# Four split pieces of projection weights, made at other places and in other scratch tiles

## The chip, the cores and the metric

One core of a Trainium2 chip runs the whole kernel. The metric is device microseconds (us) of one execution, and lower is better. The kernel before takes 2753.55 us, the median of three runs (2752.94 to 2757.86).

## The reference

One layer of a streaming encoder over 2048 tokens of width 1024, all in float32. Cut to what matters here:

```
xn = rms_norm(x, mix_norm_g)
aq|ak|av|mq|mk|mv|mo|i|f|ga|gm = xn @ w_in
A = chunk_band_attention(aq, ak, av, rel_bias)          # own chunk and 8 before, 8 heads of 64
M = sigmoid(mo) * rms_norm(mlstm_chunkwise(silu(conv(mq|mk)), mv, i, f))   # 4 heads of 128
y = sigmoid(ga) * (A @ w_att_proj) + sigmoid(gm) * (M @ w_mlstm_proj)
x = x + y @ w_out
x = x + relu(rms_norm(x) @ w_up)^2 @ w_down
out = rms_norm(x)
```

## The kernel before

**Products.** A float32 product is made of three matmuls on a high and a low part of each operand (high x high, high x low, low x high). So every weight tile is split ahead of its use: ScalarE casts the tile to the high part (L685), VectorE subtracts that from the tile (L687). The result lies in one of three tiles `wsp`. The raw tile comes over the SP queue (L583, L644) into one of four tiles `wraw`. Activations are split likewise (L1654 or L1656 on ScalarE, L1659 or L1661 on VectorE) into tiles `r`.

**Quads.** Most large products are done in groups called quads: seven products instead of eight of a two by two block product, with sums and differences of the weight blocks as operands. One quad is 7 weight tiles of 24 matmuls each (L853). PE adds products into shared banks, so between them the copies L2289 (ScalarE, bank to a `ctx` tile) and the sums L2297 (VectorE) must have read a bank before PE writes it again. The sums of weight blocks are made either on the way (L704) or ahead of time by `sum_w` (L560, its subtraction is L575), which loads four pieces into four `ctx` tiles and stores the sums to the tensor `wsum`.

**Order of the program.** The sequence comes from `dense` (L956). The 2048 tokens are four blocks of 512; the first span holds blocks 0 and 1, the second blocks 2 and 3. With the times of the profiled execution:

- 0 to 489 us: input products of blocks 0 and 1, attention and the recurrence of these blocks between them.
- 489 to 640 us: four quads of gates (`GATES`).
- 640 to 775 us: the projections of block 1 (L768 to L770), whose merge with the gates (L1450 loads a gate over SP, L1458 and L1468 multiply and add on VectorE) feeds the output quads; then two output quads (L2511 adds their banks to x).
- 775 to 1201 us: eleven quads of input products of blocks 2 and 3 (`IN_ORDER`).
- 1201 to 1501 us: eight quads of the up projection of the first span (`after_up`).
- 1501 to about 1976 us: the down projection of the first span (L768 to L770), with attention (L1845, L1876, L1818) and the recurrence of blocks 2 and 3 between its matmuls.
- from 1976 us: `project_quads` (L1225), the projections of blocks 2 and 3, which reads split weights ready made from DRAM (`load_split`, L586); then the output, up and down quads of the second span.

**The four pieces.** `project_quads` needs the seven split operands of two quads. They are made long before by `sum_split` (L594) in four pieces: two quads, each in two halves of the columns. One piece loads four 128x512 blocks into four `ctx` tiles (L602), makes four differences on VectorE (L612), and for each of seven operands runs `split_keep` (L628): it takes two scratch tiles, casts the high part on ScalarE (L634), subtracts the low part on VectorE (L636), and stores both to DRAM (tensors `wsplit`, L2550); a scratch tile is free again when its store has landed. The table `KEPT_SUMS` (L64) says at which quad a piece is begun: -4 to -1 are the four gate quads, 0 to 10 the input quads, 11 to 18 the up quads. The pieces have a low priority, so they run where the engines have room.

**Pools.** `ctx` has 16 tiles and serves almost everything: block sums, loads, bank copies. `sc` has 4 tiles (two scores tiles for each half of an attention head). Attention uses `sc` until about 440 us and again from about 1540 us; between these, `sc` serves `norm_mid` (L555), which squares the residual stream for the second norm (load L2584, square L2586 on ScalarE, sum L2590 on VectorE), 16 tiles in the first span; its result is needed at 1347 us.

**The order on each engine.** A planner (`Flow`) walks through all threads with costs and priorities and hands out the tiles; a second pass (`Order`) lists the recorded instructions anew, each engine by due times, with margins for transfers. Each engine then runs its list in order. So the table and the pool of the scratch tiles reach far beyond their own instructions: whoever takes a tile later waits for whoever had it before.

Of the kernel before, what the change touches and what calls it, by code (L numbers as in the profile page):

```python
# [60 lines left out]
ORDER = (0, 1, 3, 2, 5, 4, 6)  # L61
PLAIN, APART = (0, 1, 2, 3, 4, 5, 6), (0, 2, 3, 1, 5, 4, 6)
CHAIN = (1, 0, 3, 5, 6, 2, 4)
KEPT_SUMS = {-4: (0, 0), -3: (0, 1), 8: (1, 0), 17: (1, 1)}  # L64
N_RING = 8
LAST = (3, 1)

# [149 lines left out]
def act_ns(n, ps=False, ap=0):  # L217
    return (51 if ps else 93) + 0.834 * n + 93 * ap


def dve_ns(n):
    return 70 + 1.042 * n
# [162 lines left out]
class Layer:  # L385
# [242 lines left out]
    def split_keep(self, x, n, h, read):  # L628

        fl = self.fl  # L630
        got = yield "get", self.ctx, 2
        hi, lo = (t[:, :512] for t in got)
        yield "act", act_ns(512)
        self.nc.scalar.copy(hi.bitcast(F32R), x)  # L634
        yield "dve", dve_ns(512)
        self.nc.vector.tensor_sub(lo.bitcast(F32R), x, hi)  # L636
        fl.set(read)
        for y, (t, u) in enumerate(zip(got, (hi, lo))):
            fl.spawn(self.store(self.ws[n].ap().bitcast(F32)[:, y, h * 512:h * 512 + 512], u,
                                self.ws_ev[n][2 * h + y], self.ctx, t), 3)  # L640

    def split_w(self, i, src, raw, sent=None, keep=None):
        yield "sp", 1750, 2000
# [312 lines left out]
    def dense(self):  # L956
# [59 lines left out]
        for i, name in enumerate(GATES):  # L1016
            if i - 4 in KEPT_SUMS:
                q, h = KEPT_SUMS[i - 4]
                fl.spawn(self.sum_split(Q_P + q, h), 3)
# [16 lines left out]
        for i, name in enumerate(IN_ORDER):  # L1036
            if i in KEPT_SUMS:
                q, h = KEPT_SUMS[i]
                fl.spawn(self.sum_split(Q_P + q, h), 3)
# [12 lines left out]
        for s in range(NS):  # L1052
# [7 lines left out]
            for i in range(N_F):  # L1060
                if s == 0 and len(IN_ORDER) + i in EARLY_SUMS:
                    fl.spawn(self.sum_w(EARLY_SUMS[len(IN_ORDER) + i]), 3)
                if s == 0 and len(IN_ORDER) + i in KEPT_SUMS:
                    q, h = KEPT_SUMS[len(IN_ORDER) + i]
                    fl.spawn(self.sum_split(Q_P + q, h), 3)
# [1985 lines left out]
```

## Time and profile before

| | us |
|---|---|
| median of the runs | 2753.55 |
| the profiled execution | 2757.34 |
| its span on the core | 2755.5 |
| PE busy | 2739.9 (99%) |
| VectorE busy | 2069.5 (75%) |
| ScalarE busy | 1509.4 (55%) |
| clock of PE granted over the span | 0.998 |

PE is busy for all but 15.6 us of the span, and some 8 us of these lie outside the stretch from 480 to 2100 us. A busy PE does not mean that PE is at its peak, since matmuls overlap and a matmul at a lower clock is busy for longer. A better measure in the stages that hold nothing but matmuls of 512 columns is their count in a window: a full window of 25 us has 112 of them.

### The profile page before, as it was taken

How to read it: one execution, taken by the hardware profiler on the slowest of the kernel's cores; microseconds unless marked ns; L12 is line 12 of the kernel's file. 1: busy time of each engine (PE TensorE's matmuls, PEld its weight loads, DVE VectorE, ACT ScalarE, POOL GpSimd, SP SyncE). 2: the span in 40 equal slices, each digit the busy share in tenths (PEclk: the TensorE clock that was granted, in tenths of full speed). 3: DMA queues.
4: the chain of work that ended last, by engine and by line, in shares of the span. 5: the costliest groups of instructions: out<-in, count | busy, mean ns of one | idle time of the engine just before them, and what ended most of it. 6: DMA issues, size and time to landing. Idle time of an engine off the chain costs nothing.

```text
span 2755.5 us, 38840 instructions
## 1 busy us (share of the span) xinstructions
PE 2739.9 (99%) x13006; PEld 2280.4 (83%) x13006; DVE 2069.5 (75%) x3873; ACT 1509.4 (55%) x2665; POOL 52.9 (2%) x101
## 2 busy tenths in 40 slices
PE   9999999999999999999999999999999999999999
PEld 7888888888778888887888888888888888888888
DVE  7795798777996767876677788889898656555566
ACT  5664576644454545584556565566435655554444
POOL 0010001000000000000000000000000000000000
PEclk9999999999999999999999999999999999999999
DMA  8977759889756589489889998987967667776564
GB/s 291 290 227 251 234 168 309 282 278 340 243 205 233 172 301 328 142 273 320 285 312 312 313 287 254 269 252 248 329 243 260 210 220 258 237 248 220 194 221 163
DMA packets 339417, 704.09 MB, mean 256 GB/s; under 512 B 37992, under 2 KB 68880, under 8 KB 337424
## 3 DMA queue, kind: packets, MB, share of 16 engines
q1 hardware_dynamic: 339072, 701.60, 77.0%
q8 instruction: 102, 1.67, 0.3%
q14 instruction: 99, 0.81, 0.1%
q10 hardware_dynamic: 144, 0.01, 0.0%
HBM read 483.60 MB, written 217.86 MB: 255 GB/s over the span
## 4 chain that ended last, share of the span: by engine, by line
PE 97%; DMA 1%; DVE 1%; ACT 0%; issue 0%; SPq 0%; POOL 0%; ACTq 0%
PE bank L853 45%; PE bank L768 12%; PE bank L770 12%; PE bank L769 12%; PE bank L884 3%; PE bank L1258 3%; PE bank L1845 2%; PE bank L1818 2%; PE bank L1876 2%; PE bank L2131 0%; PE bank L2132 0%; PE bank L2116 0%; PE bank L2130 0%; DMA r<-mfar 0%; PE bank L935 0%; DMA tmp<-mixa 0%
## 5 line engine op out<-in xcount | busy, mean ns | idle before, releaser
L853 PE MATMUL bank<-r,wsp 128*128 128x512 f32 x5544 | 1268.1, 390 | 6.0 <-ACT ctx L2289 3.5
L853 PEld LDWEIGHTS bank<-r,wsp 128*128 128x128 f32 x5544 | 1040.7, 188 | 225.5 <-ACT ctx L2289 3.9
L687 DVE TENSOR_TENSOR wsp<-wraw,wsp 128x1024 fp32r<-128x1024 f32 x442 | 540.0, 1222 | 353.7 <-ACT wsp L685 337.4
L685 ACT CAST wsp<-wraw 128x1024 fp32r<-128x1024 f32 x442 | 465.5, 1053 | 539.8 <-PE bank L853 226.5
L768 PE MATMUL bank<-r,wsp 128*128 128x512 f32 x1328 | 529.2, 399 | 0.0
L769 PE MATMUL bank<-r,wsp 128*128 128x512 f32 x1328 | 519.1, 391 | 0.0
L770 PE MATMUL bank<-r,wsp 128*128 128x512 f32 x1328 | 518.6, 391 | 0.0
L770 PEld LDWEIGHTS bank<-r,wsp 128*128 128x128 f32 x1328 | 249.3, 188 | 53.1
L768 PEld LDWEIGHTS bank<-r,wsp 128*128 128x128 f32 x1328 | 249.6, 188 | 45.4
L769 PEld LDWEIGHTS bank<-r,wsp 128*128 128x128 f32 x1328 | 249.9, 188 | 44.6
L2297 DVE TENSOR_TENSOR ctx<-bank,ctx 128x512 f32<-128x512 f32 x186 | 126.7, 687 | 104.2 <-PE bank L853 101.2
L1659 DVE TENSOR_TENSOR r<-r 128x512 fp32r<-128x512 f32 x251 | 165.8, 687 | 14.3 <-ACT r L1654 14.0
L1654 ACT CAST r<-r 128x512 fp32r<-128x512 f32 x251 | 149.9, 622 | 28.9 <-DMA r<-u 24.6
L2289 ACT COPY ctx<-bank 128x512 f32<-128x512 f32 x186 | 107.8, 582 | 90.6 <-PE bank L853 73.9
L1860 ACT ACTIVATE sc<-sc,scs 128x640 f32<-128x640 f32 (+4 forms) x128 | 97.4, 762 | 75.4 <-DVE scs L1857 69.5
L1851 DVE CUSTOM_DVE_ANT_0 sc<-bank,bias 128x320 f32<-128x320 f32 (+3 forms) x240 | 103.4, 461 | 11.9 <-PE bank L1845 10.5
L1881 DVE TENSOR_TENSOR r<-bank,r 128x512 fp32r<-128x512 f32 (+1 forms) x168 | 97.0, 595 | 20.0 <-ACT r L1879 18.8
L1879 ACT CAST r<-bank 128x512 fp32r<-128x512 f32 (+1 forms) x168 | 82.3, 517 | 48.6 <-PE bank L1876 46.7
L2628 ACT ACTIVATE ctx<-ctx 128x512 f32<-128x512 f32 x96 | 60.5, 630 | 77.2 <-DVE ctx L2297 77.2
L1818 PE MATMUL bank<-r,r 128*128 128x512 f32 x336 | 94.9, 363 | 0.0
L704 DVE TENSOR_TENSOR wraw<-wraw,wraw 128x1024 f32<-128x1024 f32 x76 | 92.3, 1218 | 0.6
L1845 PE MATMUL bank<-r,r 128*128 128x320 f32 (+3 forms) x480 | 85.5, 305 | 0.0
(295 smaller groups left out, 2975.7 us busy)
## 6 DMA issues: line engine op xcount, KB each, us to landing
wraw<-in_wf SPq DMA_DIRECT2D x178, 512.0 KB, 4.8
wraw<-wsum SPq DMA_DIRECT2D x136, 512.0 KB, 4.0
r<-u SPq DMA_DIRECT2D x224, 256.0 KB, 4.3
wraw<-in_w SPq DMA_DIRECT2D x71, 512.0 KB, 5.2
ctx<-in_wf SPq DMA_DIRECT2D x128, 256.0 KB, 5.1
u<-ctx SPq DMA_DIRECT2D x128, 256.0 KB, 3.1
wsum<-ctx SPq DMA_DIRECT2D x112, 256.0 KB, 4.6
u<-tmp SPq DMA_DIRECT2D x96, 256.0 KB, 4.0
```

The costliest lines, as they stand in the source:

```text
L685: nc.scalar.copy(w[:, 0], raw)
L687: nc.vector.tensor_sub(w[:, 1], raw, w[:, 0].bitcast(F32))
L768: mm(ps, lh, rh, start=first, stop=False)
L769: mm(ps, lh, rl, start=False, stop=False)
L770: mm(ps, ll, rh, start=False, stop=last)
L853: mm(ps, wv[:, x, k, n], a[:, y], start=new and k == 0 and x == y == 0, stop=k == 3 and x == 1, skip_group_check=True)
L1654: self.nc.scalar.copy(dst[:, 0], src)
L1659: self.nc.vector.tensor_sub(dst[:, 1], src, dst[:, 0].bitcast(F32))
L1818: nc.tensor.matmul(acc[:, :, c0:c0 + w], st, sl[:, :, o:o + w], start=n == 0, stop=n == total - 1)
L1845: nc.tensor.matmul(bks[x][:, :w], q[:, y, i * P:(i + 1) * P], kf[:, f * P + x * w:f * P + x * w + w], start=y == 0, stop=y == 1)
L2289: nc.scalar.copy(t[:, o:o + 512], ps)
L2297: nc.vector.tensor_add(t[:, o:o + 512], ps, t[:, o:o + 512])
```

## The change

Two things change. The table begins the four pieces at the third gate quad and at the input quads 3, 6 and 8, instead of at gate quads 0 and 1, input quad 8 and up quad 6. And `split_keep` takes its two scratch tiles from `sc` instead of `ctx` (a tile of that pool is a pair, the 640 wide tile and a small one; the first 512 columns of the wide one are used). The four tiles that hold the loaded blocks stay in `ctx`. No instruction is added or taken away.

```
-KEPT_SUMS = {-4: (0, 0), -3: (0, 1), 8: (1, 0), 17: (1, 1)}
+KEPT_SUMS = {-2: (0, 0), 3: (0, 1), 6: (1, 0), 8: (1, 1)}
...
     def split_keep(self, x, n, h, read):
         fl = self.fl
-        got = yield "get", self.ctx, 2
-        hi, lo = (t[:, :512] for t in got)
+        got = yield "get", self.sc, 2
+        hi, lo = (t[0][:, :512] for t in got)
         yield "act", act_ns(512)
         self.nc.scalar.copy(hi.bitcast(F32R), x)
         yield "dve", dve_ns(512)
         self.nc.vector.tensor_sub(lo.bitcast(F32R), x, hi)
         fl.set(read)
         for y, (t, u) in enumerate(zip(got, (hi, lo))):
             fl.spawn(self.store(self.ws[n].ap().bitcast(F32)[:, y, h * 512:h * 512 + 512], u,
-                                self.ws_ev[n][2 * h + y], self.ctx, t), 3)
+                                self.ws_ev[n][2 * h + y], self.sc, t), 3)
```

**First place: the SP queue at the end of the projections of block 1** (about 686 to 704 us). L1450 loads a gate, L644 a raw weight tile, L2214 a block of the output quads' operand, L2498 a block of x. Before:

```order
L644 DMA wraw_64<-in_wf 128x1024
L2214 DMA ctx_121<-yp 128x512
L644 DMA wraw_65<-wsum 128x1024
L1450 DMA tmp_109<-gate 128x512
L1450 DMA tmp_108<-gate 128x512
L2214 DMA ctx_119<-yp 128x512
L644 DMA wraw_67<-wsum 128x1024
L1450 DMA tmp_106<-gate 128x512
L1450 DMA tmp_108<-gate 128x512
```

With the change:

```order
L644 DMA wraw_67<-wsum 128x1024
L1450 DMA tmp_110<-gate 128x512
L1450 DMA tmp_108<-gate 128x512
L644 DMA wraw_66<-wsum 128x1024
L2214 DMA ctx_124<-yp 128x512
L1450 DMA tmp_111<-gate 128x512
L1450 DMA tmp_109<-gate 128x512
L644 DMA wraw_64<-in_wf 128x1024
L2214 DMA ctx_115<-yp 128x512
L2498 DMA ctx_117<-in_xt 128x512
L644 DMA wraw_65<-wsum 128x1024
L2498 DMA ctx_122<-in_xt 128x512
```

The last two gate loads stood behind the raw tile `wraw_67`; now they stand ahead of `wraw_64`, which is three raw weight tiles earlier in the same sequence of weights.

VectorE at the end of the same stage (about 706 to 714 us): L1458 and L1468 merge the last gates, L2227 makes sums of the output quads' operands, L1661 their low parts, L687 that of a weight tile. Before:

```order
L687 TENSOR_TENSOR wsp_62<-wraw_66,wsp_62 128x1024
L2511 TENSOR_TENSOR ctx_113<-bank_134,ctx_113 128x512
L1661 SCALAR_TENSOR_TENSOR r_70<-ctx_117,r_70 128x512
L687 TENSOR_TENSOR wsp_63<-wraw_64,wsp_63 128x1024
L1458 SCALAR_TENSOR_TENSOR tmp_106<-tmp_106,bank_131 128x512
L1458 SCALAR_TENSOR_TENSOR tmp_108<-tmp_108,bank_130 128x512
L1468 TENSOR_TENSOR ctx_126<-tmp_106,tmp_107 128x512
L1468 TENSOR_TENSOR ctx_114<-tmp_108,tmp_111 128x512
L2227 TENSOR_TENSOR ctx_127<-ctx_120,ctx_126 128x512
L2227 TENSOR_TENSOR ctx_123<-ctx_125,ctx_114 128x512
L2227 TENSOR_TENSOR ctx_120<-ctx_121,ctx_120 128x512
```

With the change:

```order
L687 TENSOR_TENSOR wsp_63<-wraw_64,wsp_63 128x1024
L1661 SCALAR_TENSOR_TENSOR r_80<-ctx_113,r_80 128x512
L1661 SCALAR_TENSOR_TENSOR r_81<-ctx_112,r_81 128x512
L1661 SCALAR_TENSOR_TENSOR r_85<-ctx_125,r_85 128x512
L2251 SCALAR_TENSOR_TENSOR tmp_110<-tmp_110,gcol,bias_97 128x512
L2251 SCALAR_TENSOR_TENSOR tmp_111<-tmp_111,gcol,bias_97 128x512
L1468 TENSOR_TENSOR ctx_126<-tmp_107,tmp_106 128x512
L2266 TENSOR_TENSOR tmp_108<-tmp_110,tmp_111 128x512
L2227 TENSOR_TENSOR ctx_120<-ctx_126,ctx_125 128x512
L2251 SCALAR_TENSOR_TENSOR ctx_119<-ctx_119,gcol,bias_96 128x512
L2227 TENSOR_TENSOR ctx_126<-ctx_124,ctx_126 128x512
L1661 SCALAR_TENSOR_TENSOR r_82<-ctx_120,r_82 128x512
```

All L1458 and the other merges (L1468) now stand ahead of the weight tile `wsp_63`; the last merge, `ctx_126`, still stands behind it, and behind three low parts L1661 and two steps (L2251) that normalize x for the input quads.

**Second place: ScalarE in the second up quad** (about 1253 to 1270 us). Before:

```order
L685 CAST wsp_61<-wraw_67 128x1024
L2289 COPY ctx_115<-bank_131 128x512
L2289 COPY ctx_112<-bank_130 128x512
L685 CAST wsp_63<-wraw_64 128x1024
L2289 COPY ctx_126<-bank_133 128x512
L2628 ACTIVATE ctx_126<-ctx_126 128x512
L2632 ACTIVATE ctx_126<-ctx_126 128x512
L2289 COPY ctx_120<-bank_129 128x512
```

With the change:

```order
L685 CAST wsp_63<-wraw_66 128x1024
L2289 COPY ctx_126<-bank_129 128x512
L2289 COPY ctx_113<-bank_132 128x512
L685 CAST wsp_61<-wraw_67 128x1024
L2289 COPY ctx_122<-bank_130 128x512
L2289 COPY ctx_112<-bank_133 128x512
L685 CAST wsp_62<-wraw_65 128x1024
L2289 COPY ctx_127<-bank_129 128x512
```

The bank copies stand about one weight cast earlier, and they go to other `ctx` tiles.

**Third place: ScalarE where the first piece is split** (before about 501 to 505 us, with the change in the third gate quad, about 560 us). Before:

```order
L634 CAST ctx_113<-ctx_123 128x512
L1578 ACTIVATE tmp_110,r_q<-tmp_110 128x512
L2289 COPY ctx_115<-bank_128 128x512
L634 CAST ctx_125<-ctx_119 128x512
L1578 ACTIVATE tmp_107,r_q<-tmp_107 128x512
L685 CAST wsp_62<-wraw_64 128x1024
```

With the change:

```order
L634 CAST sc_98<-ctx_116 128x512
L685 CAST wsp_63<-wraw_64 128x1024
L2289 COPY ctx_117<-bank_130 128x512
L634 CAST sc_102<-ctx_123 128x512
L2289 COPY ctx_113<-bank_133 128x512
L634 CAST sc_98<-ctx_114 128x512
L685 CAST wsp_61<-wraw_66 128x1024
L2289 COPY ctx_127<-bank_129 128x512
```

The scratch of one operand comes back for the next but one: `sc_98` is written again one weight cast later.

The list of each engine changes well beyond these places. On PE the matmuls keep their order, but for single ones, until the end of the up projection; from there on attention and the down projection are interleaved otherwise.

More of the change, by code (lines that the diff above doesn't have):

```diff
@@ L63 @@
 CHAIN = (1, 0, 3, 5, 6, 2, 4)
-KEPT_SUMS = {-4: (0, 0), -3: (0, 1), 8: (1, 0), 17: (1, 1)}
+KEPT_SUMS = {-2: (0, 0), 3: (0, 1), 6: (1, 0), 8: (1, 1)}
 N_RING = 8
@@ L630, in split_keep @@
         fl = self.fl
-        got = yield "get", self.ctx, 2
-        hi, lo = (t[:, :512] for t in got)
+        got = yield "get", self.sc, 2
+        hi, lo = (t[0][:, :512] for t in got)
         yield "act", act_ns(512)
@@ L639, in split_keep @@
             fl.spawn(self.store(self.ws[n].ap().bitcast(F32)[:, y, h * 512:h * 512 + 512], u,
-                                self.ws_ev[n][2 * h + y], self.ctx, t), 3)
+                                self.ws_ev[n][2 * h + y], self.sc, t), 3)
     def split_w(self, i, src, raw, sent=None, keep=None):
```

## The prediction

> **What bounds the kernel now.** I read the busy times first, then PE's waits from 480 to 2100 us (the first piece begins at 473 us, the change's last effect is on the quads after 1976 us), then windows of 25 us.
>
> ```profile
> span 2755.5 us, 38840 instructions
> PE 2739.9 (99%) x13006; PEld 2280.4 (83%) x13006; DVE 2069.5 (75%) x3873; ACT 1509.4 (55%) x2665; POOL 52.9 (2%) x101
> ...
> PE bank L853 <- ACT ctx L2289: 3.5, 1, 3.5
> PE bank L853 <- ACT r L1656: 1.3, 1, 1.3
> PE bank L1553 <- POOL r_far L1585: 0.7, 1, 0.7
> PE bank L1258 <- ACT sc L1296: 0.7, 1, 0.7
> PE bank L853 <- DVE r L1659: 0.5, 1, 0.5
> PE bank L853 <- DVE r L1661: 0.4, 1, 0.4
> PE bank L853 <- DVE tmp L1458: 0.3, 1, 0.3
> ```
>
> PE sets the time. The change takes no matmul away, so it can only win back what PE loses now: seven waits of 7.4 us in all (columns: us in total, times, longest). A wait costs more than its idle time if the clock falls behind it, so I count matmuls in windows (length; then busy us and count of PE, weight loads, VectorE, ScalarE, POOL; granted clock; DMA share; GB/s).
>
> ```profile
> 675.00:700.00 25.00, 25.00 (x112) 20.68 (x111) 20.84 (x33) 11.18 (x16) 0.00 (x0) 1.00 0.68 225
> 700.00:725.00 25.00, 22.98 (x92) 17.86 (x91) 25.00 (x40) 10.85 (x15) 0.00 (x0) 0.93 0.86 299
> 1200.00:1225.00 25.00, 24.53 (x107) 19.75 (x107) 20.79 (x31) 22.14 (x36) 0.00 (x0) 1.00 0.83 278
> 1250.00:1275.00 25.00, 21.54 (x89) 17.37 (x88) 11.48 (x16) 10.79 (x16) 0.00 (x0) 0.93 0.79 268
> 1975.00:2000.00 25.00, 24.91 (x109) 20.00 (x108) 19.77 (x34) 12.24 (x22) 0.00 (x0) 1.00 1.04 410
> 2000.00:2025.00 25.00, 24.31 (x108) 19.81 (x107) 22.32 (x37) 6.37 (x11) 0.00 (x0) 1.00 0.67 240
> ```
>
> A full window has 112 matmuls, so one is worth 25/112 = 0.2232 us. Short of that: 20 matmuls = 4.46 us at 700 us (place C), 5 = 1.12 us at 1200 us (D), 23 = 5.13 us at 1250 us (E), 3 + 4 = 1.56 us at 1975 to 2025 us (F): 12.3 us. The 0.7 us of L1553 (place B, 493 us) come on top. That is the whole prize.
>
> **The change part by part.** The same 28 casts, 28 differences of low parts, 16 differences of blocks, 56 stores (and the loads of the blocks) run in both kernels, so nothing is added or removed:
>
> ```profile
> L634 ACT CAST ctx<-ctx x28: 601/621/663, 501.0 to 1597.0; 128x512 fp32r<-128x512 f32 x28
> L636 DVE TENSOR_TENSOR ctx<-ctx,ctx x28: 671/684/694, 503.9 to 1607.8; 128x512 fp32r<-128x512 f32 x28
> L612 DVE TENSOR_TENSOR ctx<-ctx,ctx x16: 669/686/694, 518.6 to 1580.0; 128x512 f32<-128x512 f32 x16
> L2550 SPq DMA_DIRECT2D wsplit<-ctx x56: 319/405/1052, 501.9 to 1610.5; - x56
> DMA to landing us min/median/max: 2.6/5.2/10.1
> ```
>
> Per piece that is 7 x 0.62 = 4.3 us of ScalarE, 7 x 0.68 + 4 x 0.69 = 7.5 us of VectorE, and 14 x 0.41 = 5.7 us of SP's issue for the stores. Lying beside full PE windows (VectorE 20.84 of 25 us at 675) it costs PE nothing. Without that cover, up to its 7.5 us of VectorE would show. What the change moves is who waits for which tile, so I go by places.
>
> *E, taken as gone: 5.1 us.* The chain of waits there:
>
> ```profile
> 1254.88 0.69 DVE ctx L575
> 1255.59 5.43 DMA wsum<-ctx
> 1261.11 0.59 ACT ctx L2289
> ```
>
> The bank copy L2289 had its bank long before. It waited for its `ctx` tile, which `sum_w` held until a store of 5.43 us had landed; PE stood 3.46 us, and the slower clock behind it makes up the rest of 5.13. In the change two scratch tiles per operand come from `sc` and not from `ctx`, the copies at this place stand one weight cast earlier and go to other tiles, whose former use is, in my reading of the lists, over 4 us done. So I take all 5.1; if another copy meets a tile still being stored, all of it remains (0).
>
> *C, half gone: 2.2 us.*
>
> ```profile
> 703.01 0.32 SPq L1450
> 703.39 3.68 DMA tmp<-gate
> 709.46 1.20 DVE tmp L1458 x2
> 710.65 1.20 DVE ctx L1468 x2
> 712.39 1.28 DVE ctx L2227 x2
> 713.67 0.61 DVE r L1661
> ```
>
> The last gate came at 703.39 + 3.68 = 707.07 us; VectorE then had to merge (two L1458, two L1468) and to form sums and low parts before PE could go on. The load now stands three raw weight tiles earlier. A weight tile feeds 24 matmuls, 24 x 0.2232 = 5.36 us, so it lands some 16 us earlier, and the merges but one stand ahead of the last weight tile's L687. But VectorE is full in this window (25.00 of 25 us), its sum of work is the same, and the last merge stands behind three L1661 and two L2251, some 5 x 0.65 = 3.3 us more. Before, two L1458 and one more L1468 stood there (1.20 + 0.60 = 1.8 us). So the load is no longer last, but VectorE's queue is. Bounds 0 and 4.46; I take half.
>
> The clock at C is a matter of its own:
>
> ```profile
> 712.00:714.00 2.00, 0.73 (x2) 0.30 (x2) 2.00 (x4) 2.00 (x4) 0.00 (x0) 1.00 1.03 401
> 714.00:716.00 2.00, 1.68 (x6) 1.41 (x7) 2.00 (x5) 0.82 (x2) 0.00 (x0) 0.85 1.05 383
> 716.00:718.00 2.00, 2.00 (x6) 1.52 (x6) 2.00 (x5) 1.61 (x4) 0.00 (x0) 0.50 1.04 396
> ```
>
> Waits of 0.3, 1.3 and 0.4 us brought the clock to 0.85 and then 0.50, so 2.0 us of idle time cost 4.46. [...]
>
> *D, half gone: 0.6 us.* PE waited 0.47 us for an operand's low part (L1659), one of many splits that run until 1222 us. In the change all those of the first operands stand ahead of the weight cast at 1214 us. Against it: `norm_mid` needs `sc` as well, and with the pieces there it comes later. Before:
>
> ```profile
> L2586 ACT ACTIVATE sc<-sc x14: 614/628/639, 722.7 to 839.9; 128x512 f32<-128x512 f32 x14
> L2590 DVE TENSOR_TENSOR bias<-bias,sc x14: 681/686/694, 811.3 to 840.6; 128x512 f32<-128x512 f32 x14
> 1175.00:1200.00 25.00, 25.00 (x112) 20.71 (x111) 20.91 (x31) 22.45 (x37) 0.00 (x0) 1.00 0.82 259
> ```
>
> By the lists these 16 squares move from 722 to 840 us to some 1105 to 1224 us: 10.0 us of ScalarE and 11 us of VectorE next to D, where ScalarE has 22.45 of 25 us, while the third piece (4.3 and 7.5 us) leaves it. Bounds 0 and 1.12, half taken. At 800 us the squares leave a full VectorE; no PE wait stands there, so nothing is won.
>
> *B and F: 0.* L1553 comes 20 matmuls earlier at B, as do the steps that feed it; +-0.7. F waits for a copy of `project_quads` itself (L1296), which the change leaves; at best 1.56 are won.
>
> *From 1501 to 1937 us: 0.*
>
> ```profile
> 1501.00:1937.00 436.00, 436.00 (x2362) 373.71 (x2361) 366.13 (x974) 270.30 (x601) 13.76 (x36) 1.00 0.88 271
> 1955.74 0.37 ACT L1825 COPY tmp<-bank 128x256 f32<-128x256 f32 x1 [3.73 <-DVE ctx L2665]
> 1976.03 26.51 PE L1258 MATMUL bank<-r,wsp 128*128 128x512 f32 x114
> ```
>
> The fourth piece leaves this stretch, which is full already and gains nothing. Attention starts later there, and the last L1818 stands 36 matmuls (8.0 us) nearer to the first L1258. Its copy L1825 waited 14 us for its tile before, so that move has cover. Without it, about 4 us would show: 8.0 less the some 4 us that I count between the last operand and its use.
>
> *New waits: 1.7 us of loss.* The lists change everywhere from 490 us on, and each of about a hundred PE windows can meet what happened at E. From none (0) to one more stall of E's size (5.1); I take a third.
>
> **Sum:** 5.1 + 2.2 + 0.6 - 1.7 = 6.2 us. The profiled execution took 2757.34 us (span 2755.5, 1.8 around it) and would come to 2751.1. It stands 3.8 us above the median of the three runs, 2753.55, which gives **2747.3 us**.
>
> **The rivals.**
>
> *Larger gain.* If C to F all go and nothing new comes: 2753.55 - 12.3 = 2741.3, with a small rest 2742.5. For it: PE has no idle time in the full windows at 675 and 1175 us, so stalls are single accidents. Against: VectorE is full at C.
>
> *No change.* `ctx` is used 16 deep and `sum_w` still stores from it; the stall of E comes back at another quad (-7.9 + 5.1) or C remains whole and a late attention tail costs its 4 us (-5.7 + 4): about 2752. For it: what is moved earlier, loads of the pieces included, holds `ctx` tiles at other quads.
>
> *Slower.* Only two pairs of scratch fit into the four `sc` tiles. A pair is held for the cast, the difference and the store, 0.62 + 0.68 + 5.2 = 6.5 us at the median and 11.4 us at the longest landing of 10.1; it is wanted again after one or two weight tiles, 5.4 to 10.7 us. ScalarE runs its list in order, so a cast L634 that waits holds up the bank copies and weight casts queued behind it. PE's cover is one weight tile less a copy and a sum, 5.36 - 1.3 = 4 us. From a landing of about 9 us on, PE waits. If three of four pieces meet one such landing, at E's price: 3 x 5.13 = 15.4 - 7.9 = +7.5, so 2761.0. Waits for stores now (idle before L634, then before L636; us, times):
>
> ```profile
>   DMA gate<-ctx: 3.7, 2
> ...
>   DMA wsplit<-ctx: 1.9, 1
> ```
>
> For it: both wait for stores even with 16 tiles. Against it: PE had no wait at L853 between 490 and 700 us in spite of them.
>
> That the change does not do what it says can be left out: the lists show all four pieces done at 1085 us and the scratch in `sc`.
>
> **How the numbers follow.** A measurement of this kernel can tell about 0.2% (5.5 us) from no change: below 2748.0 is faster, above 2759.1 slower. Forecast (2744 to 2751): 0.42, two thirds of it faster (0.28), a third the same (0.14). Larger gain: 0.20, faster. No change: 0.20, the same. Slower: 0.18. So faster 0.48, same 0.34, slower 0.18. The range reaches from below the full prize, 2740, to the slower case, 2761.
>
> **What would show it.** Right: the window of E has about 112 matmuls and no wait of L853 for L2289 anywhere; that of C has about 102, a single wait for L1661 or L1656, and its gate loads land before 695 us; `norm_mid`'s squares lie past 1100 us; from 1976 us on all is as before. The larger gain: both windows full. No change: a wait for a copy L2289 behind a store at another quad, or 92 matmuls at C again. Slower: L634 idle for `wsplit<-sc` by several us and a PE wait within 6 us behind it, three times. I would be wrong if PE's lost time came up where no window has any now, above all between 775 and 1200 us or past 1940 us.

## The result and the profile after

The changed kernel takes 2744.97 us, the median of six runs (2744.52 to 2745.26), against 2752.59 us of the kernel before, six runs beside them: 7.6 us less, a ratio of 0.9969 with the interval 0.9956 to 0.9982. The forecast of 2747.3 us was right in direction and 2.3 us too high; the time lies inside its own 2744 to 2751. A second set gave 2745.23 against 2754.55 us, 0.9967 (0.9954 to 0.9979). The profiled execution took 2744.52 us, its span 2742.7 us.

PE's waits of the changed kernel between 480 and 2100 us (us in total, times, longest):

```profile
PE bank L884 <- ACT ctx L2289: 1.6, 1, 1.6
PE bank L853 <- DVE r L1661: 0.8, 2, 0.4
```

Seven waits have become three. Its windows of 25 us at the places where the kernel before lost matmuls, and at 1050 us (columns as in the prediction):

```profile
700.00:725.00 25.00, 24.11 (x104) 19.02 (x103) 24.11 (x37) 7.16 (x9) 0.00 (x0) 1.00 0.85 255
1050.00:1075.00 25.00, 23.40 (x104) 19.04 (x103) 18.84 (x25) 13.55 (x20) 0.00 (x0) 1.00 0.96 340
1200.00:1225.00 25.00, 25.00 (x112) 20.67 (x111) 22.85 (x34) 18.54 (x30) 0.00 (x0) 1.00 0.93 324
1250.00:1275.00 25.00, 25.00 (x112) 20.70 (x111) 16.50 (x20) 14.22 (x22) 0.00 (x0) 1.00 0.87 305
1975.00:2000.00 25.00, 25.00 (x112) 20.68 (x111) 15.69 (x26) 5.84 (x10) 0.00 (x0) 1.00 0.70 262
2000.00:2025.00 25.00, 25.00 (x112) 20.69 (x111) 24.82 (x43) 14.60 (x27) 0.00 (x0) 1.00 0.92 335
```

D, E and F have their full 112. C lacks 8 where it lacked 20, and a new place, G at 1050 us, lacks 8 where nothing was lost. So 39 of 55 missing matmuls are back: 39 x 0.2232 = 8.7 us, and with the 0.7 us of L1553 (place B) 9.4 us.

The last gate load of C was issued at 680.1 us, and none took more than 5.1 us to land. At C the chain of waits shows what is left:

```profile
703.87 1.80 DVE r L1661 x3
705.68 1.32 DVE tmp L2251 x2
707.00 0.60 DVE ctx L1468
...
708.12 0.69 DVE ctx L2227
...
710.08 0.60 DVE r L1661
...
711.20 0.68 DVE r L1661
```

No load stands in it any more. The last merge L1468 comes behind three L1661 and two L2251, and PE then waits 0.41 us twice for low parts: VectorE's queue.

At G the chain is of another kind:

```profile
1064.21 0.70 DVE ctx L2297
...
1065.25 0.40 ACT tmp L2385
1065.65 0.95 ACT wsp L685
1066.60 0.49 ACT ctx L2289
...
1067.13 8.02 PE bank L884 x34
```

The bank copy L2289 stands on ScalarE behind a weight cast, and that behind two casts L2385 that wait for a sum of VectorE. The copy writes the `ctx` tile that the casts read (`ctx_124` in the list), so it could not have gone ahead of them into that tile.

The pieces ran where the lists said, and their stores landed in time:

```profile
L634 ACT CAST sc<-ctx x28: 610/622/629, 536.3 to 1067.6; 128x512 fp32r<-128x512 f32 x28
...
DMA to landing us min/median/max: 3.3/4.8/8.0
```

### The profile page after: what moved, and what is told of

Same layout as the page of the kernel before. It is cut to its first block, busy times and chain, and to the rows that moved or that the text cites. A ratio compares the mean times of both kernels' runs of the same rounds, so it can differ in the third digit from the quotient of the medians.

```text
span 2742.7 us, 38893 instructions
## 1 busy us (share of the span) xinstructions
PE 2734.2 (100%) x13006; PEld 2278.4 (83%) x13006; DVE 2072.4 (76%) x3873; ACT 1508.6 (55%) x2665; POOL 50.5 (2%) x101
## 4 chain that ended last, share of the span: by engine, by line
PE 99%; DVE 0%; ACT 0%; issue 0%; ACTq 0%
PE bank L853 46%; PE bank L768 12%; PE bank L770 12%; PE bank L769 12%; PE bank L1258 3%; PE bank L884 3%; PE bank L1845 2%; PE bank L1818 2%; PE bank L1876 2%; PE bank L2131 1%; PE bank L2132 1%; PE bank L2116 1%; PE bank L2130 1%; PE bank L935 0%; PE bank L1919 0%; PE bank L974 0%
## 5 line engine op out<-in xcount | busy, mean ns | idle before, releaser
L853 PE MATMUL bank<-r,wsp 128*128 128x512 f32 x5544 | 1263.8, 390 | 0.9 <-DVE r L1661 0.8
L853 PEld LDWEIGHTS bank<-r,wsp 128*128 128x128 f32 x5544 | 1038.7, 188 | 218.5 <-DVE r L1661 1.7
L687 DVE TENSOR_TENSOR wsp<-wraw,wsp 128x1024 fp32r<-128x1024 f32 x442 | 540.1, 1222 | 348.7 <-ACT wsp L685 329.7
L1654 ACT CAST r<-r 128x512 fp32r<-128x512 f32 x251 | 149.8, 622 | 24.1 <-DMA r<-u 20.9
L2289 ACT COPY ctx<-bank 128x512 f32<-128x512 f32 x186 | 107.9, 581 | 81.3 <-PE bank L853 71.9
L1818 PE MATMUL bank<-r,r 128*128 128x512 f32 (+1 forms) x336 | 94.5, 362 | 0.0
L704 DVE TENSOR_TENSOR wraw<-wraw,wraw 128x1024 f32<-128x1024 f32 x76 | 92.4, 1218 | 0.5
```

The lines of the kernel that those rows point to most:

```text
L687: nc.vector.tensor_sub(w[:, 1], raw, w[:, 0].bitcast(F32))
L853: mm(ps, wv[:, x, k, n], a[:, y], start=new and k == 0 and x == y == 0, stop=k == 3 and x == 1, skip_group_check=True)
L1654: self.nc.scalar.copy(dst[:, 0], src)
L1818: nc.tensor.matmul(acc[:, :, c0:c0 + w], st, sl[:, :, o:o + w], start=n == 0, stop=n == total - 1)
L2289: nc.scalar.copy(t[:, o:o + 512], ps)
```

## The experiments

Each kernel is judged by its time beside runs of the kernel before, and by the matmuls that its windows lack, counted in all windows of 25 us from 500 to 1325 us and from 1950 to 2100 us that hold matmuls of 512 columns alone. The kernel before lacks 55, so a kernel that lacks n should differ from it by (n - 55) x 0.2232 us.

| kernel | table | scratch | median us | before us | ratio (interval) | lacks: window x matmuls | by count | measured |
|---|---|---|---|---|---|---|---|---|
| before | -4, -3, 8, 17 | ctx | 2752.59 | | 1 | 700 x20, 1200 x5, 1250 x23, 1975 x3, 2000 x4: 55 | | |
| changed | -2, 3, 6, 8 | sc | 2744.97 | 2752.59 | 0.9969 (0.9956, 0.9982) | 700 x8, 1050 x8: 16 | -8.7 | -7.6 |
| e1 | -2, 3, 6, 8 | ctx | 2774.50 | 2754.55 | 1.0073 (1.0060, 1.0086) | 700 x4, 925 x7, 950 x33, 1125 x8, 1175 x12, 1200 x71, 1225 x11: 146 | +20.3 | +20.0 |
| e2 | -4, -3, 8, 17 | sc | 2761.57 | 2754.55 | 1.0025 (1.0015, 1.0035) | 700 x8, 1975 x79, 2000 x1: 88 | +7.4 | +7.0 |
| e3 | as before, one sum in sc | ctx | 2748.39 | 2754.55 | 0.9979 (0.9970, 0.9988) | 675 x2, 700 x12, 1950 x2, 1975 x4: 20 | -7.8 | -6.2 |
| e5 | -4, -3, 8, 12 | sc | 2753.35 | 2754.51 | 0.9998 (0.9989, 1.0007) | 700 x9, 1200 x1, 1300 x1, 1975 x34: 45 | -2.2 | -1.2 |
| e6 | -4, -3, 6, 8 | ctx | 2774.57 | 2754.51 | 1.0072 (1.0060, 1.0085) | 675 x2, 700 x17, 1050 x10, 1175 x36, 1200 x7, 1225 x53, 2000 x12: 137 | +18.3 | +20.1 |
| e7 | changed, two sc tiles fewer | sc | 2748.47 | 2754.51 | 0.9979 (0.9970, 0.9988) | 700 x9, 925 x1, 1000 x2, 1050 x11: 23 | -7.1 | -6.0 |
| e8 | -2, 3, 5, 9 | sc | 2751.74 | 2754.51 | 0.9989 (0.9980, 0.9998) | 700 x8, 975 x2, 1000 x6, 1200 x20, 1975 x5: 41 | -3.1 | -2.8 |
| e9 | -4, -3, 6, 8 | sc | 2751.59 | 2753.98 | 0.9990 (0.9981, 0.9999) | 700 x8, 1050 x17, 1975 x20: 45 | -2.2 | -2.4 |
| e10 | -2, 2, 4, 6 | sc | 2755.06 | 2753.98 | 1.0002 (0.9993, 1.0011) | 700 x7, 875 x5, 975 x6, 1000 x5, 1025 x15, 1975 x7: 45 | -2.2 | +1.1 |
| e11 | changed again | sc | 2745.23 | 2754.55 | 0.9967 (0.9954, 0.9979) | 700 x8, 1050 x8: 16 | -8.7 | -9.3 |
| e12 | -2, 3, 6, 9 | sc | 2754.28 | 2754.55 | 0.9999 (0.9990, 1.0008) | 700 x8, 1050 x10, 1175 x19, 1975 x20: 57 | +0.4 | -0.3 |

The count comes from one profiled execution of each kernel, the time is a median. Even so it explains each of these times within 2 us but that of e10, whose profiled execution (2751.78 us) was the fastest of its eleven, with a median of 2755.06. The fairer comparison is profiled execution against profiled execution. Before's stood at 2757.34 us and had 2.1 us of waits at L2105 (about 460 us) and 0.7 us at L1553 (place B), both outside the counted windows. With the waits at these two lines added, the count is within 1.7 us of each profiled execution, e10 with 0.5 among them, but for e6 (2.7). So nearly the whole difference among these kernels is stalls of PE at a handful of places, as the prediction assumed.

**e1: the table alone.**

```
-KEPT_SUMS = {-4: (0, 0), -3: (0, 1), 8: (1, 0), 17: (1, 1)}
+KEPT_SUMS = {-2: (0, 0), 3: (0, 1), 6: (1, 0), 8: (1, 1)}
```

> The new table alone; the scratch of the pieces stays in the ctx tiles. If the early begin of the pieces is what counts (it takes work and loads out of the later quads), all of the gain comes: 7.6 us less than before, 0.9972. If the freed ctx tiles count, nothing comes: within 2 us of before, and a wait of the matmuls L853 for a copy L2289 of some 3.5 us stands at one of the quads. If the gain is nothing but that the old lists happened to hold one bad meeting of a copy and a store (place E), then any new lists win about 5 us: 0.998.

20 us slower, which no theory had. The worst window, and the chain of waits that ends its longest stall (PE waits 15.1 us for an operand's cast L1654):

```profile
1200.00:1225.00 25.00, 9.82 (x41) 7.40 (x40) 13.25 (x20) 16.28 (x26) 0.00 (x0) 0.77 0.80 262
```

```profile
1211.27 0.35 ACT ctx L634
1211.62 5.23 DMA mfar<-ctx
1216.85 0.02 issue
1216.88 0.70 DVE ctx L636
1217.58 0.02 issue
1217.61 0.70 DVE ctx L612
1218.32 2.46 DMA ctx<-x
1220.81 0.73 ACT ctx L2254
...
1222.83 0.69 DVE ctx L2266
1223.54 0.63 ACT r L1654
```

It is a ring through `ctx`. The low part L636 of a piece waits 5.23 us for its scratch tile, from which another store is still running. Behind it the piece's difference L612 is late, and the load of an operand of the up projection (from x) waits for that. At 1200 us, where the up projection begins, `ctx` is asked for by the pieces, the operands and the block sums at once. So the early table is not a gain by itself. E went away in it too (1250 us is full), as it did in every altered kernel, so a full window there proves neither half of the change.

**e2: the scratch alone.**

```
-        got = yield "get", self.ctx, 2
-        hi, lo = (t[:, :512] for t in got)
+        got = yield "get", self.sc, 2
+        hi, lo = (t[0][:, :512] for t in got)
...
-                                self.ws_ev[n][2 * h + y], self.ctx, t), 3)
+                                self.ws_ev[n][2 * h + y], self.sc, t), 3)
```

> The scratch in sc alone; the table stays the old one, so the pieces begin at gate quads 0 and 1, input quad 8 and up quad 6. If the freed ctx tiles count, all of the gain comes: 7.6 us less, 0.9972, with no wait of L853 for L2289 at 1250 us. If the early begin counts, nothing comes: within 2 us of before. If any new lists win: about 5 us, 0.998.

7 us slower, which no theory had either. D and E are gone and C has 104, so some 40 matmuls come back; whether the freed `ctx` tiles bring them or only the new lists is not shown, as e3 wins 35 with other lists. But `project_quads` loses 79. Its window and waits:

```profile
1975.00:2000.00 25.00, 13.85 (x33) 8.61 (x33) 24.71 (x42) 11.27 (x19) 0.00 (x0) 0.59 0.88 287
```

```profile
PE bank L1258 <- ACT r L1654: 5.6, 2, 4.6
PE bank L1258 <- DVE r L1659: 5.6, 1, 5.6
```

With the old table the fourth piece wants `sc` while attention uses it. Its last casts run at 1987 us, its low parts L636 stand between the operand splits on a full VectorE (24.71 of 25 us), and attention's last copy L1825 is at 1973.5 us, 14 us behind the first L1258. In the kernel before, that copy was 20 us ahead of it.

Neither half of the change is a gain: +20.0 and +7.0 us alone, -7.6 together.

**e3: place E's cause by itself.** The block sums for one quad, whose tile the copy at E waited for, are made in `sc`. It is the third quad of the down projection, not of the up projection; the program asks for them at the first up quad.

```
-            got = yield "get", self.ctx, 4
-            a, b, c, d = (x[:, :512] for x in got)
+            pool = self.sc if q in SUM_SC else self.ctx; got = yield "get", pool, 4
+            a, b, c, d = ((x[0] if q in SUM_SC else x)[:, :512] for x in got)
...
-            fl.put(self.ctx, *got)
+            fl.put(pool, *got)
```

with `SUM_SC = (N_Q - N_F + 2,)`.

> The kernel before with one thing changed: the block sums for the third up quad (sum_w, which held the ctx tile that PE waited for at place E) are made in the four sc tiles. Pieces, table and their scratch are as before. If place E is a copy that meets a ctx tile held by that sum's store, the window 1250 to 1275 us gets its 112 matmuls and the time falls by 5.1 us (0.9981), while C, D and F lose what they lost before. If the tile is only a symptom (PE would wait there for something else, such as the weights behind it), E keeps more than 2 us and the time falls by less than 3 us.

```profile
700.00:725.00 25.00, 23.31 (x100) 18.25 (x99) 25.00 (x38) 11.81 (x16) 0.00 (x0) 1.00 0.88 310
1250.00:1275.00 25.00, 25.00 (x112) 20.72 (x111) 16.35 (x19) 14.31 (x22) 0.00 (x0) 1.00 0.88 311
```

E is full, and the time falls by 6.2 us where 5.1 were expected. But the edit moved more than the pool. With tiles from `sc`, which attention leaves at about 440 us, the planner makes these sums far earlier:

```profile
L575 DVE TENSOR_TENSOR sc<-sc,sc x8: 680/684/695, 441.6 to 512.4; 128x512 f32<-128x512 f32 x8
```

In the kernel before the same eight stand between 1089.9 and 1256 us, and hold four `ctx` tiles there. So e3 takes the tile and the work away from E at once, and does not separate the two. That the copy waited for the store of this sum rests on the trace of before: both have the tile `ctx_126` in the lists, and the copy starts 0.1 us after the store has landed. e3 agrees with it and is no proof by itself. D went too, where the sum held its four tiles as well. C got 8 of its 20 back (6 net of the 2 that are lost at 675 us), though nothing was touched there but the lists. Part of what the change won at C may be no more than a new list.

**e4: the kernel before, once more.** Nothing is changed.

> The kernel before once more, for a second profile. If the stalls are set by the lists, C, D, E and F show the same counts of matmuls within 3 of the first profile (92, 107, 89, 109 and 108), and only what lies before 480 us differs. If they hang on how long single transfers take in one execution, some of them are missing or half as long, and the time differs by as much.

One execution, 2758.28 us. The same waits stand at the same places, but not with the same cost, and one is new:

```profile
1250.00:1275.00 25.00, 21.55 (x83) 17.25 (x82) 12.15 (x16) 11.89 (x18) 0.00 (x0) 0.86 0.72 246
1975.00:2000.00 25.00, 22.88 (x100) 18.68 (x101) 20.50 (x34) 12.87 (x23) 0.00 (x0) 1.00 1.03 404
```

```profile
PE bank L1258 <- DMA wsp<-wsplit: 2.1, 1, 2.1
```

The first profile had the waits of L2105 for another transfer instead. So C, D and E belong to the lists, and a few us on top depend on single transfers. Both profiled executions of before (2757.34 and 2758.28 us) lie at the upper end of its runs (2750.48 to 2758.00 over all sets), and so the first profiles of before and of the change differ by 12.8 us and the medians by 7.6.

**e5: the scratch in sc, of the table only the fourth piece moved.** The edit of e2, and

```
+KEPT_SUMS = {-4: (0, 0), -3: (0, 1), 8: (1, 0), 12: (1, 1)}
```

> The scratch in sc, and of the table only the fourth piece moved: it begins at up quad 1 instead of up quad 6, the first three begin where they did before. The scratch alone lost 17.6 us at project_quads, where the fourth piece and attention shared the four sc tiles. If that meeting is the whole of its loss, this kernel is 5 to 9 us faster than before (0.997 to 0.998) with no wait of L1258 for an operand's cast over 1 us. If the early begin of the other three is needed as well, more than 5 us of stalls stand elsewhere and it is not faster than before.

As fast as before. The loss at `project_quads` is 34 matmuls in place of 79, and the piece is not in it any more (its last cast is at 1283 us). What is late is attention: its last L1825 is at 1962.2 us, 3 us ahead of the first L1258, and PE waits 5.5 us for an operand's cast behind the merge with it; a load of 8.22 us (`mixa`) stands in that chain too. So without the fourth piece at that place somewhat under half of e2's loss is still there. In all other kernels but e2 that copy is 20 to 40 us ahead. What makes attention end so late here, with no piece beside it, stays open.

**e6: the scratch in ctx, the third and fourth piece at input quads 6 and 8.**

```
+KEPT_SUMS = {-4: (0, 0), -3: (0, 1), 6: (1, 0), 8: (1, 1)}
```

> The scratch in ctx, as before; of the table only the third and the fourth piece are moved, to input quads 6 and 8 as in the change; the first two begin where they did before. If what made the table alone 20 us slower is that two pieces with 6 ctx tiles and more each stand in the input quads beside the operands of the up projection, it is at least 10 us slower than before, with PE waits of several us near 1200 us. If the first two pieces' place was the cause, it is within 3 us of before.

As expected, 20.1 us slower. PE's largest wait and the chain that ends one of its stalls:

```profile
PE bank L853 <- ACT ctx L2289: 13.4, 3, 6.1
```

```profile
1232.63 5.67 DMA wsplit<-ctx
1238.31 0.02 issue
1238.33 0.63 ACT ctx L634
...
1238.98 0.70 DVE ctx L636
...
1239.70 0.70 DVE ctx L612
...
1240.95 0.59 ACT ctx L2289
```

The cast L634 waits 5.67 us for its scratch tile's store, and the bank copy L2289, for which PE waits, is queued behind it and a further cast. That is the mechanism of the prediction's slower case, at 1232 us, but with scratch from `ctx`.

**e9: the same table with the scratch in sc**, the edits of e6 and e2 together.

> The table with only the third and fourth piece moved (input quads 6 and 8, the first two at gate quads 0 and 1 as before), and the scratch in sc; the same table with ctx scratch was 20 us slower than before. If the freed ctx tiles are what that table needs, its stalls between 1175 and 1250 us (89 matmuls, 19.9 us) go, and it is at least 4 us faster than before and 20 us faster than with ctx scratch. If attention's late end at project_quads comes with the first two pieces' place (they stood there in both kernels that had it), the quads from 1975 us on lose 5 us or more and it is no faster than before.

2751.59 against 2774.57 us: the pool of the scratch is worth some 23 us with this table, and the 96 matmuls that 1175 to 1250 us lacked (36, 7 and 53) are all there. Yet it beats before by 2.4 us only, as 20 matmuls (4.5 us) are lost at 1975 us and 17 at 1050 us. So the first theory has the pool's worth right and not the 4 us against before; the second has the loss at 1975 us nearly right and its cause wrong, for attention ends 25 us ahead of the first L1258 here, as in the changed kernel.

**e7: one pair of scratch tiles in place of two.** Two `sc` tiles are taken with the first piece and given back with the last, and nobody uses them.

```
-        s = slice(h * 512, h * 512 + 512)
+        s = slice(h * 512, h * 512 + 512); self.held = (yield "get", self.sc, 2) if q == Q_P and h == 0 else self.held
...
-        fl.put(self.ctx, *got)
+        fl.put(self.ctx, *got); fl.put(self.sc, *(self.held if q == Q_P + 1 and h == 1 else ()))
```

> The changed kernel with two of the four sc tiles kept from everyone while the pieces run, so that each operand waits until the stores of the one before have landed. If two pairs were near their limit (the slower case of the prediction, where a pair that is late by some us stops PE), half of them costs at least 3 us against the changed kernel. If the pieces have slack, as the lists run them whenever the engines have room, it is within 2 us of the changed kernel: some 7 us faster than before.

3.5 us slower than the changed kernel by the medians (2748.47 against 2744.97), 1.6 us by the differences from the runs of before beside each (-6.0 and -7.6), and still faster than before. The pieces end at 1160 us instead of 1068. No window lacks more than 11 matmuls and no PE wait names a piece's cast L634, its difference L636 or its store, so even one pair did not stop PE as the slower case had it. The answer lies between the two expectations, and how much of it is the pair and how much the new lists stays open.

**e8 and e12: the fourth piece one quad later, with and without the third one earlier.** The changed kernel with

```
+KEPT_SUMS = {-2: (0, 0), 3: (0, 1), 5: (1, 0), 9: (1, 1)}
```

and with

```
+KEPT_SUMS = {-2: (0, 0), 3: (0, 1), 6: (1, 0), 9: (1, 1)}
```

> The changed kernel with the third piece one quad earlier and the fourth one quad later (input quads 5 and 9). The changed kernel's new stall of 1.8 us at 1065 us (a bank copy behind a weight cast, behind casts of its own tile) lies while the fourth piece holds four ctx tiles. If the pieces cause it, it goes: 1.8 us less than the changed kernel, 0.9965 of before. If it is the lists' own, it stays or moves, and the time is within 2 us of the changed kernel either way up.

> The changed kernel with the fourth piece alone one quad later (input quad 9). Moving it and the third piece (one quad earlier) took away the stall at 1065 us but brought one of 20 matmuls at 1215 us, beside the operands of the up projection. If the late fourth piece is what brought that one, it is here too: no wait at 1065 us, 4.5 us lost near 1215 us, 2 to 4 us slower than the changed kernel. If the early third piece did, the changed kernel's time comes or up to 1.8 us less.

e8 has no stall at 1065 us, but 20 matmuls less at 1200 us, and is 2.8 us faster than before, 4.8 us short of the changed kernel by the differences from before; both of its expectations missed. e12 keeps the loss at 1050 us (10), loses 19 at 1175 us and 20 at 1975 us, and is as fast as before, which is worse than either expectation had it. Both have a stall beside the operands of the up projection: in e8 PE waits 1.8 us for an operand's cast (at 1218 us), in e12 2.3 us for a bank copy behind operand casts on ScalarE (at 1191 us). That the fourth piece causes G is not shown: G went with the third piece's place.

**e10: the last three pieces earlier.** The changed kernel with

```
+KEPT_SUMS = {-2: (0, 0), 2: (0, 1), 4: (1, 0), 6: (1, 1)}
```

> The changed kernel with the last three pieces one or two quads earlier (input quads 2, 4 and 6), scratch in sc. All pieces are then done before the quads of 1046 us on, where the changed kernel's new stall (1.8 us) stands and where VectorE is fullest. If earlier pieces are better by themselves, it is as fast as the changed kernel or up to 3.6 us faster (both of its stalls gone). If the places of the changed kernel are just a good draw among lists, it is 2 to 8 us slower than the changed kernel, with stalls at other places.

As fast as before (1.1 us over it, inside the interval), where the changed kernel is 7.6 to 9.3 us under it. There is no stall at 1050 us, but 31 matmuls are lost in windows between 875 and 1050 us and 7 at 1975 us. Earlier is not better by itself, and the distance to the changed kernel is a little more than the 2 to 8 us that were expected if that kernel is a good draw among lists.

**e11: the changed kernel once more.** Nothing is changed.

> The changed kernel once more, for a second profile and more runs of it. If its two stalls are set by the lists, the windows from 700 and from 1050 us have 104 matmuls each within 3 again, and all others their full count; the gain is 7 to 9 us. If the profiled execution was a lucky one, stalls of other places turn up, as they did between the two profiles of before (6 us of waits for single transfers there), and the gain is under 6 us.

The same two windows lack the same 8 matmuls each, and 2745.23 us is the time, 9.3 us under before. The gain belongs to the lists and not to a lucky execution.

## Why the prediction was right

**The bound.** The prediction took the gain from seven PE waits of the kernel before, and from matmuls counted in full windows. Both held: the count gave the difference from before within 2 us for the changed kernel and nine of ten altered ones. One of its signs of being wrong did come, lost time between 775 and 1200 us (G), but no more of it than the allowance for new waits.

**E, 5.1 us, taken as gone.** It went. The cause that was named, a bank copy whose tile a sum's store still held, is in both traces of before. Why it went is less than the prediction made of it: E is full in all altered kernels, also in e1 and e6, where the scratch stayed in `ctx`. It was one bad meeting in one set of lists (e6 has another such wait of a bank copy in the window before), and no run shows that the freed tiles or the earlier pieces were needed to be rid of it.

**C, half of 4.46 us.** 12 of 20 came back, 2.7 us against 2.2. Half of the bounds was a choice between 0 and 4.46, so the nearness is in part luck. The rest is the queue that was named: three L1661 and two L2251 ahead of the last merge. What the earlier gate loads did is not separated from the new list, for C has 95 to 108 in all altered kernels. It lacks 17 or more only where the first two pieces stand at gate quads 0 and 1 and the scratch is in `ctx` (before, e6), and 4 to 9 where either of the two is changed; e3, with neither changed, lacks 12.

**D, half of 1.12 us, and F and B, nothing.** Here the sum was too small. D went whole though ScalarE is as full as feared (24.93 of 25 us at 1175 us). The squares of `norm_mid` ran from 1098 to 1182 us and were over before D; the prediction had read them from the lists as lasting until 1224. F went whole, 1.56 us, and B, 0.7 us. "F waits for a copy of `project_quads` itself, which the change leaves" was the step that failed: the copy was left, but nothing makes PE wait for it now. In the kernel before, that copy (L1296, at 2002.59 us) needs a tile `sc` that a sum of VectorE reads (`tmp<-tmp,sc`), and this sum stands behind two others that wait for PE's banks:

```profile
1999.85 0.69 DVE L1316 SCALAR_TENSOR_TENSOR ctx<-ctx,bank 128x512 f32<-128x512 f32 x1 [5.14 <-PE bank L1258]
2001.21 0.69 DVE L1316 SCALAR_TENSOR_TENSOR ctx<-ctx,bank 128x512 f32<-128x512 f32 x1 [0.67 <-PE bank L1258]
2001.82 0.68 DVE L1316 SCALAR_TENSOR_TENSOR tmp<-tmp,sc 128x512 f32<-128x512 f32 x1
```

In the changed kernel it stands one place earlier:

```profile
1988.04 0.69 DVE L1316 SCALAR_TENSOR_TENSOR ctx<-ctx,bank 128x512 f32<-128x512 f32 x1 [7.66 <-PE bank L1258]
1988.65 0.68 DVE L1316 SCALAR_TENSOR_TENSOR tmp<-tmp,sc 128x512 f32<-128x512 f32 x1
```

The copy then starts 24.7 us after the first L1258 and not 26.6, and PE does not wait. That is one step in the planner's list, which nothing in the prediction foresaw, so F was won by luck.

**From 1501 to 1937 us, nothing.** The last L1818 does stand 8.3 us nearer to the first L1258 (26.0 us ahead, before 34.3), and its copy L1825, which had waited 14 us for its turn, follows at once, 25.7 us ahead instead of 20.3. So the cover that the prediction counted on was there. It was not there in e2 and e5. It does not keep these quads full by itself: in e9 the copy is 24.9 us ahead, and 20 matmuls are lost.

**New waits, 1.7 us.** One came, G, with 8 matmuls or 1.8 us. It was an allowance with no place to it, so its size is luck.

**The sum.** 23 + 12 + 5 + 7 - 8 = 39 matmuls and B make 9.4 us, where 6.2 were forecast; the medians fell by 7.6 and 9.3. The forecast is near because what it missed at C, D, F and B (some 3 us) all lay on one side and is small; F and B came with the new lists and not from anything that it named.

**The rivals.** The slower case put its price on the two pairs in `sc`, and that did not come: e7 halved them for 1.6 to 3.5 us. Its mechanism, a cast L634 behind its tile's store with a bank copy behind it, is real (e6), but in `ctx` with pieces late among the input quads. The attention tail was priced at some 4 us and put with "no change"; in e2, where the fourth piece came on top, what stood there cost 17.9 us, and in e5 7.6. And the prediction went through the change by places, never asking what each of its two halves would do alone. Both lose (e1, e2). In the traces the early table suffers from the want of `ctx` tiles near 1200 us, which scratch in `sc` relieves (e1 against the changed kernel, e6 against e9). Scratch in `sc` suffers where a piece meets attention in `project_quads` (e2); but with the pieces done long before (e5) 34 matmuls are still lost there, so this second need is shown in part only.

No kernel tried beats the changed one.

## What to carry to other kernels

Where PE is at 99% of the span, count its matmuls in windows: the missing ones, times the pitch of one, gave differences of 2 to 20 us between kernels to within 2 us, and each lack has a place and a chain that can be read. A change that moves work between pools and one that moves it in time are to be thought of together: ask who uses the new pool at the new time, and who uses the old pool there. Where a planner makes the lists, one step of one piece in the table (e12) brought stalls of 4 us each at places that it never touched and took the whole gain away. So a gain of this size belongs to one set of lists, and is to be measured and not argued.

## What the runs showed of the hardware

The same wait did not cost the same in two executions. At E PE stood for 3.46 us in the first profile of before and 3.45 us in the second, but 23 matmuls were lost in one and 29 in the other, with a granted clock of 0.93 and 0.86 over the window: 1.3 us between them. Behind the wait the clock was 0.88, 0.50 and 0.76 in the first, in slices of 2 us, and 0.58 over the 4 us from 1258 us, then 0.50 and 0.64 in slices of 2 us in the second. At G, 1.60 us of idle time in one piece left the clock at full:

```profile
1066.00:1068.00 2.00, 0.87 (x4) 0.74 (x5) 2.00 (x4) 2.00 (x5) 0.00 (x0) 1.00 0.95 351
1068.00:1070.00 2.00, 2.00 (x11) 1.62 (x9) 2.00 (x5) 1.75 (x3) 0.00 (x0) 1.00 1.21 322
```

and it cost 8 matmuls, 1.8 us, little more than itself. At C of the kernel before, 2.0 us in three pieces brought the clock to 0.50 and cost 4.46. So the price of a wait of 1.5 to 3.5 us lay between once and some twice its length. Short waits cost more than their length with no slow clock at all: the windows of D and F in the kernel before and of C in the changed one have a clock of 1.00 and lost 1.12, 1.56 and 1.79 us for 0.47, 0.78 and 0.89 us without a busy PE. What else is lost around them is not shown; it is a price that the prediction, which named the clock alone, left out. Nor is it shown why the clock fell at C and E but not at G, and why it was low for longer in the second profile of E than in the first.

By the profile a matmul L853 of the kernel before took 0.39 us on average, at a pitch of 0.2232 us in full windows, so they overlap. At C, in the slice at 716 us with the clock of 0.50, PE was busy for all of the 2.00 us with 6 matmuls, where a slice of 2 us at a clock of 1.00 without a wait has 10 or 11.
